# Sums of squares of x and mem taken from their columns by products with ones

## The chip, the cores and the metric

The kernel runs on one core of one Trainium2 chip. The metric is the device time of one execution in microseconds (us). Engines: PE (TensorE; PEld is its weight load), ACT (ScalarE), DVE (VectorE), POOL (GpSimd), SP (SyncE, which here only issues loads and stores).

## What is computed

One decoder layer on 256 tokens of width 1024, in float32. What matters here is its first step: x and 256 memory tokens mem are normalised by rows (RMSNorm) and projected.

```
def rmsnorm(x, g):
    y = x * rsqrt(mean(x * x, axis=-1) + EPS)
    return y * g

h = rmsnorm(x, mix_norm_g)                      # (256, 1024)
proj = h @ w_in                                 # q, k, v of two attentions, mem q, 3 branch gates
mem_n = rmsnorm(mem, mem_norm_g)                # (256, 1024)
mk, mv = split(mem_n @ w_mem_kv)
# three attentions; their outputs, times sigmoid(gates), are merged and projected
x = x + merged @ w_out
x = x + ConvFFN(rmsnorm(x, ffn_norm_g))
```

## The kernel before

Every weight is split into a rounded part (hi, by ACT) and the rest (lo, by DVE or by a DMA of POOL that adds), and so is every activation. A product of the reference is three products on PE: hi by hi, hi by lo, lo by hi. Weights come from DRAM in pieces of up to 512 KB into 6 raw slots; a raw slot is free when its lo part is made, and there are 6 slots for the hi and lo parts, free when PE has used them.

x is loaded twice: transposed (`x_cols`, tile sig, 8 blocks of 128x256), scaled by the gain and split into T_x, which PE multiplies; and by rows (tile xs, 2 blocks of 128 tokens), from which come the sums of squares and to which the layer's output is added. mem likewise: `mem_cols` gives T_mem, the rows of mem only the sums. The 1/rms of a row is applied after the projection. A row's sum of squares is made in two halves by ACT and DVE with an accumulator (tile junk), added on DVE, raised to -1/2 on POOL, and kept in tile rs. For x it is also spread along the free axis into tile R by a product of ones with a diagonal matrix (tp_R).

The program's order is written by a planner (class Order) as the kernel is built: each task is a sequence of stages on engines, with times from a cost table and priorities, and the planner writes the stage that can start first. Each engine then runs its instructions in that order, and waits where an operand is late. The order of projections is va, vd, qa, gate 0, ka, gates 1 and 2, mv, mk and so on; tiles are named after them (raw_, hi_, lo_, acc_). While PE would wait early on, the planner writes fillers (warm, products of ones with ones). The planner's cost of an fp32 product on PE is its columns times four:

```
            return n * (4 if out_parts(args) == 128 else 2) / 2400.0
```

All loads except the adding ones are issued by SP, in the order of the string LOADS at the start, and then piece by piece as slots come free (L301).

Of the kernel before, what the change touches and what calls it, by code (L numbers as in the profile page):

```python
# [11 lines left out]
F32 = mybir.dt.float32  # L12
# [3 lines left out]
AF = mybir.ActivationFunctionType  # L16
ALU = mybir.AluOpType
# [3 lines left out]
P = 128  # L21
S = 256
NT = 2
D = 1024
KT = D // P
DH = 64
# [5 lines left out]
EPS = 1e-6  # L32
# [5 lines left out]
RAW = 3  # L38
PRIO_SCALE = 11
CUTS = (0, 1, 2, 4, 8)  # L40
LOADS = "x01 g w x12 w x24 w x46 w x68 w r0 r1 c"
SUMS = (4, 130, 5)
BACK = (1.5, 2.0)
SLACK = 0.6
MEM_AT = 16.0
PRIO_SPLIT = (0, 0, 0, 12, 12, 22, 35, 40)
MAGIC = 12582912.0
TWO_PI = float(np.nextafter(np.float32(2.0 * np.pi), np.float32(0.0)))
# [185 lines left out]
def tile_layer(ctx: ExitStack, tc: tile.TileContext, io, out):  # L234
    nc = tc.nc
    od = Order(nc)
    pe, act, dve, pool = od.pe, od.act, od.dve, od.pool

    cpool = ctx.enter_context(tc.tile_pool(name="cpool", bufs=1))
# [8 lines left out]
    def bank_free(tag):  # L248

        return lambda: users[tag][-BANKS[tag]]["end"] if len(users[tag]) >= BANKS[tag] else 0.0  # L250

    def bank(tag, name):
        use = {"end": None}
        users[tag].append(use)
        shape = [P, 2, 512] if tag == "sc" else [P, 512]
        return ps.tile(shape, F32, tag=tag, name=name, bufs=BANKS[tag]), use
# [33 lines left out]
    at = {"unit": 0, "raw": 0, "dma": 0.0, "sw": 0.0, "lo": 0, "quiet": False}  # L290
# [94 lines left out]
    def urgency(part):  # L385
        def f():
            g = next((g for g in grains if (g.get("hi", {"end": None})["end"] is None if part == 0 else not g.get("taken"))), None)
            d = g["first"] - at["unit"]
            return PRIO_SPLIT[min(d, len(PRIO_SPLIT) - 1)] if d >= 0 else PRIO_SPLIT[0]
        return f  # L390
# [16 lines left out]
    xs = cpool.tile([P, NT, D], F32, tag="xs", name="xs")  # L407
# [6 lines left out]
    mhalf = cpool.tile([P, 8], F32, tag="mhalf", name="mhalf")  # L414
    ones = cpool.tile([P, P], F32, tag="ones", name="ones")
    R = cpool.tile([P, S], F32, tag="R", name="R")
    sq, rstd = {}, {}
# [5 lines left out]
    task = {}  # L423

    def done(*keys):

        return lambda: [task.get(k, {"end": None}) for k in keys]
# [11 lines left out]
    def sums(src, key, t, prio, parts):  # L439

        nm = f"{key}{t}"
        if (key, t) not in sq:
            sq[key, t] = npool.tile([P, 4], F32, tag="ssq", name="ssq_" + nm, bufs=4), []
        total, tasks = sq[key, t]
        for c0, c1, eng, after in parts:
            i = len(tasks)
            tasks.append(od.add(square_task(src, c0, c1, eng, total[:, i:i + 1], nm, after), prio))

    def rstd_task(key, t):

        total, tasks = sq[key, t]
        rs = rstd[key, t] = cpool.tile([P, 2], F32, tag=f"rs_{key}{t}", name=f"rs_{key}{t}")
        yield Stage("dve", lambda: tasks)
        dve.tensor_reduce(rs[:, 0:1], total[:, :len(tasks)], axis=AX.X, op=ALU.add)
        yield Stage("dve")
        dve.tensor_scalar(rs[:, 0:1], rs[:, 0:1], 1.0 / D, EPS, op0=ALU.mult, op1=ALU.add)
        yield Stage("pool")
        pool.tensor_tensor(rs[:, 0:1], rs[:, 0:1], mhalf[:, 0:1], op=ALU.pow)

    def head_scale_task(key, t):  # L460

        yield from rstd_task(key, t)
        rs = rstd[key, t]
        yield Stage("dve")
        dve.tensor_scalar(rs[:, 1:2], rs[:, 0:1], rs[:, 0:1], 1.0 / DH, op0=ALU.mult, op1=ALU.mult)

    def row_scale_task(key, t):

        d = npool.tile([P, P], F32, tag="diag", name=f"diag_{key}{t}")
        yield Stage("dve", done(("rs", key, t)))  # L470
        dve.tensor_scalar(d, ident, rstd[key, t][:, 0:1], None, op0=ALU.mult)
        yield Stage("pe", bank_free("tp"))
        pt, use = bank("tp", f"tp_R{key}{t}")
        pe.matmul(pt[:, :P], ones, d, start=True, stop=True)
        yield Stage("act", frees=[use])
        act.activation(R[:, t * P:(t + 1) * P], pt[:, :P], AF.Copy)
# [7 lines left out]
    def columns_of(key, gi, cols, prio, after):  # L484
        for k in range(KT):
            new = od.add(column_task(key, k, cols[:, k, :], gi, after(k)), prio + 0.01 * k)
            for t in range(NT):
                task[key, t, k] = new
# [96 lines left out]
    sig = apool.tile([P, 24, S], F32, tag="sig", name="sig")  # L585
# [284 lines left out]
    for nm, arg in ORDER:  # L870
# [15 lines left out]
        else:  # L886
            br, c = arg
# [172 lines left out]
    def mem_task():  # L1060
        yield Stage("pool", MEM_AT)
        nc.sync.dma_start(conv, io["conv"])
        cols = sig[:, KT:2 * KT, :]
        rows = sig[:, 2 * KT:3 * KT, :].rearrange("p a b -> p (a b)").rearrange("p (t n) -> p t n", t=NT)
        there = []
        for out_, in_ in [(cols[:, 0:4], io["mem_cols"][:, 0:4]), (cols[:, 4:8], io["mem_cols"][:, 4:8])] + \
                [(rows[:, t, :], io["mem"][t * P:(t + 1) * P, :]) for t in range(NT)]:
            nc.sync.dma_start(out_, in_)
            at["dma"] = max(at["dma"], od.t["pool"] + 1.15) + 1.5
            there.append(at["dma"] + 1.4)  # L1070
        columns_of("mem", 2, cols, 15, lambda k: there[k // 4])
        for t in range(NT):
            sums(rows[:, t, :], "mem", t, 16, [(0, 512, "act", there[2 + t]), (512, 1024, "act", there[2 + t])])
            task["rs", "mem", t] = od.add(head_scale_task("mem", t), 14)

    def keep_busy(start):

# [11 lines left out]
    with tc.manual_schedule():  # L1089
        nc.vector.memset(ones, 1.0)  # L1090
        nc.gpsimd.memset(mhalf, -0.5)
        warm = cpool.tile([P, 1], F32, tag="warm", name="warm")
        nc.scalar.activation(warm, mhalf[:, 0:1], AF.Square)
        xcol = sig[:, 0:KT, :]
        at["dma"] = 1.9
        there = {}
        for w in LOADS.split():
            if w == "g":
                nc.sync.dma_start(gcol, io["gcol"])
                at["dma"] += 0.06  # L1100
            elif w == "w":
                load(0.0, at["raw"] + 1)
            elif w == "c":
                nc.sync.dma_start(cst, io["cst"])
                nc.sync.dma_start(pos_i, io["pos"])
                nc.sync.dma_start(hg.rearrange("p k d -> p (k d)"), io["head_gains"].to_broadcast([P, 6 * DH]))
                at["dma"] += 1.4
            elif w[0] == "x":
                k0, k1 = int(w[1]), int(w[2])
                nc.sync.dma_start(xcol[:, k0:k1, :], io["x_cols"][:, k0:k1, :])  # L1110
                at["dma"] += 0.38 * (k1 - k0)
                for k in range(k0, k1):
                    there[k] = at["dma"] + 1.2
            else:
                t = int(w[1])
                nc.sync.dma_start(xs[:, t, :], io["x"][t * P:(t + 1) * P, :])
                at["dma"] += 1.5
                there["r", t] = at["dma"] + 1.3
        load(0.0)
        make_identity(nc, ident)  # L1120
        T["x"] = tpool.tile([P, KT, 2, S], F32R, tag="T8", name="T_x")
        T["mem"] = tpool.tile([P, KT, 2, S], F32R, tag="T8", name="T_mem")
        for k in od.t:
            od.t[k] = 3.2
        warm_up = ps.tile([P, 512], F32, tag="acc", name="warm_up", bufs=4)
        for i in range(WARM):
            nc.tensor.matmul(warm_up[:, :P], ones, ones, start=True, stop=True)
        for t in range(NT):
            r = there["r", t]
            sums(xs[:, t, :], "x", t, 9, [(0, 512, "act", r), (512, 1024, "dve", r)])  # L1130
            task["rs", "x", t] = od.add(head_scale_task("x", t), 8)
            task[f"R{t}"] = od.add(row_scale_task("x", t), 9)
        columns_of("x", 0, xcol, 2, lambda k: there[k])
        od.add(split_hi(), urgency(0))
        at["left"] = len(grains)
        od.add(split_lo("dve"), urgency(1))
        od.add(split_lo("sum"), 35)
        task["mask"] = od.add(mask_task(), 25)
        od.add(mem_task(), 15)
        task["rope"] = od.add(rope_task(), 18)  # L1140
        for b in range(3):
            task[("sig", b)] = od.add(sig_task(b), 28)
        od.add(spine(units), 50)
        for key in [("out", c, t, 512) for c in range(2) for t in range(NT)]:
            while key not in task:
                od.run(units[-1])
            od.run(task[key])
# [50 lines left out]
```

## Time and profile before

| | us |
|---|---|
| median of 3 runs (419.21 to 419.32) | 419.26 |
| profiled execution | 419.38 |
| its span, first to last instruction | 417.6 |
| PE busy | 407.9 |
| DVE busy | 302.7 |
| ACT busy | 269.1 |

The times of the rows below are of the profiled execution and count from the start of its span. A DMA share of 1 or more is read as full.

### The profile page before, as it was taken

The numbers are of one execution on the slowest core, as the hardware profiler recorded it, in microseconds if no ns is written. First come the engines' busy times: TensorE is split into PE (matmuls) and PEld (weight loads), VectorE is DVE, ScalarE is ACT, GpSimd is POOL, SyncE is SP. The second block draws the span as 40 slices with busy tenths as digits, with TensorE's granted clock in tenths as the row PEclk, the third lists the DMA queues.
The fourth block names the chain that finished last, engine by engine and source line by source line (L and its number), as shares of the span: only waits on it lengthen the run. The fifth ranks groups of instructions, "written<-read, shape, count | busy, mean of one in ns | idle before, by whom it ended". The sixth has DMA issues, their size and how long they took to land.

```text
span 417.6 us, 7771 instructions
## 1 busy us (share of the span) xinstructions
PE 407.9 (98%) x2968; PEld 384.0 (92%) x2968; DVE 302.7 (72%) x600; ACT 269.1 (64%) x448; POOL 62.3 (15%) x63
## 2 busy tenths in 40 slices
PE   8899999999999999999999989999999999999996
PEld 7799999989898999999889889999999999888996
DVE  2699986586786586367987999999998778545301
ACT  4699756768976665956577877766668776433300
POOL 0101534113424102322007200000000000000000
PEclk9999999999999999999999999999999999999999
DMA  6999986667677777577597659666799688664001
GB/s 198 383 374 278 317 249 157 181 167 180 146 200 162 201 208 197 131 228 239 140 290 177 162 131 287 188 187 201 230 257 222 230 220 239 204 197 150 0 2 50
DMA packets 97988, 83.12 MB, mean 199 GB/s; under 512 B 3104, under 2 KB 85920, under 8 KB 97952
## 3 DMA queue, kind: packets, MB, share of 16 engines
q1 hardware_dynamic: 95360, 73.86, 58.6%
q0 software_dynamic: 2592, 8.78, 11.7%
q8 instruction: 23, 0.38, 0.4%
q14 instruction: 13, 0.11, 0.1%
HBM read 72.80 MB, written 1.05 MB: 177 GB/s over the span
## 4 chain that ended last, share of the span: by engine, by line
PE 83%; DVE 8%; ACT 3%; DMA 2%; issue 2%; SPq 1%; DVEq 0%; ACTq 0%
PE acc_u L101 27%; PE acc_g L101 16%; PE acc_d L101 15%; PE acc_o L101 5%; PE acc_qd L101 2%; PE acc_kd L101 2%; DMA xs<-x 2%; PE acc_ba L101 2%; PE acc_bd L101 2%; PE sc L101 2%; PE po L101 2%; PE acc_mk L101 1%; PE acc_qm L101 1%; PE acc_bm L101 1%; PE acc_mv L101 1%
## 5 line engine op out<-in xcount | busy, mean ns | idle before, releaser
L101 PE MATMUL acc_u<-T_h,hi_up 128*128 128x256 f32 x512 | 91.4, 282 | 0.0
L101 PEld LDWEIGHTS acc_u<-T_h,hi_up 128*128 128x128 f32 x512 | 78.9, 189 | 0.0
L101 PE MATMUL acc_u<-T_h,lo_up 128*128 128x256 f32 x256 | 72.1, 282 | 0.0
L101 PE MATMUL acc_g<-T_x,hi_gate 128*128 128x256 f32 x384 | 71.8, 287 | 0.0
L101 PEld LDWEIGHTS acc_g<-T_x,hi_gate 128*128 128x128 f32 x384 | 59.6, 191 | 2.4 <-issue 2.2
L101 PE MATMUL acc_d<-hi_dn,gT 128*128 128x512 f32 (+1 forms) x220 | 57.0, 348 | 0.0
L101 PE MATMUL acc_g<-T_x,lo_gate 128*128 128x256 f32 x192 | 54.2, 282 | 0.0
L101 ACT ACTIVATE hi_up<-raw_up 128x1024 fp32r<-128x1024 f32 x44 | 46.0, 1054 | 4.3 <-DMA raw_up<-w_ffn_up 1.7
L101 PEld LDWEIGHTS acc_u<-T_h,lo_up 128*128 128x128 f32 x256 | 48.4, 189 | 0.0
L101 DVE TENSOR_TENSOR lo_up<-raw_up,hi_up 128x1024 fp32r<-128x1024 f32 x39 | 47.6, 1232 | 0.0
L101 DVE SCALAR_TENSOR_TENSOR y<-acc_u,conv,y 128x255 f32<-128x255 f32 x88 | 42.2, 481 | 7.3 <-ACT y L101 5.4
L101 PEld LDWEIGHTS acc_d<-hi_dn,gT 128*128 128x128 f32 x220 | 38.5, 189 | 5.5
L101 PE MATMUL acc_d<-lo_dn,gT 128*128 128x512 f32 (+1 forms) x110 | 38.3, 348 | 0.0
L101 DVE TENSOR_TENSOR lo_dn<-raw_dn,hi_dn 128x1024 fp32r<-128x1024 f32 x21 | 25.7, 1224 | 17.3 <-ACT hi_dn L101 17.3
L101 ACT ACTIVATE hi_dn<-raw_dn 128x1024 fp32r<-128x1024 f32 x22 | 23.3, 1057 | 22.4 <-PE acc_d L101 22.4
L101 PE MATMUL acc_u<-T_hu,hi_up 128*128 128x256 f32 x192 | 34.9, 284 | 2.6 <-DVE y L101 2.6
L101 PEld LDWEIGHTS acc_g<-T_x,lo_gate 128*128 128x128 f32 x192 | 36.7, 191 | 0.0
L101 DVE TENSOR_TENSOR lo_gate<-raw_gate,hi_gate 128x1024 fp32r<-128x1024 f32 x19 | 23.8, 1262 | 13.3 <-ACT hi_gate L101 12.8
L101 PEld LDWEIGHTS acc_u<-T_hu,hi_up 128*128 128x128 f32 x192 | 29.6, 189 | 2.9 <-ACT T_h L101 2.9
L101 ACT ACTIVATE y<-acc_u,conv 128x256 f32<-128x256 f32 x44 | 24.4, 561 | 10.9 <-PE acc_u L101 10.3
L101 ACT ACTIVATE hi_gate<-raw_gate 128x1024 fp32r<-128x1024 f32 x24 | 25.0, 1056 | 6.1 <-PE acc_qm L101 2.9
L101 PE MATMUL acc_u<-T_hu,lo_up 128*128 128x256 f32 x96 | 27.1, 282 | 0.0
(279 smaller groups left out, 850.9 us busy)
## 6 DMA issues: line engine op xcount, KB each, us to landing
raw_up<-w_ffn_up SPq DMA_DIRECT2D x44, 512.0 KB, 5.1
raw_gate<-w_in SPq DMA_DIRECT2D x24, 512.0 KB, 5.2
raw_dn<-w_ffn_down SPq DMA_DIRECT2D x22, 512.0 KB, 4.4
raw_wo<-w_out SPq DMA_DIRECT2D x8, 512.0 KB, 5.2
lo_gate<-raw_gate POOLq DMA_DIRECT2D x5, 512.0 KB, 5.1
lo_up<-raw_up POOLq DMA_DIRECT2D x5, 512.0 KB, 5.0
raw_vd<-w_in SPq DMA_DIRECT2D x4, 384.0 KB, 6.6
raw_qa<-w_in SPq DMA_DIRECT2D x4, 384.0 KB, 7.7
```

What stands on the lines that cost most here:

```text
L101: return fn(*args, **kw)
```

## The change

The sums of squares of x and of mem are made from the columns: ACT squares the 8 blocks in two passes of 128x1024 into a free part of sig; PE multiplies, for each of 2 row blocks and 8 column blocks, the squares as 128x128 weight with one column of ones (16 products, sums on PSUM, tile tp_s); DVE and POOL make the scales of both row blocks at once. The rows of mem aren't loaded any more. The rows of x are loaded when the planner's clock is at 110. The columns of x are issued on ACT's queue, ahead of its table load, the last four blocks in one load.

```diff
-LOADS = "x01 g w x12 w x24 w x46 w x68 w r0 r1 c"
+LOADS = "x01 g w x12 w x24 w x48 w w w c"
+ROWS_AT = 110.0
+SQUARES_AT = 12.5
...
+    def column_square_task(cols, out_, k0, k1, after):
+        yield Stage("act", after, SQUARES_AT)
+        act.activation(out_[:, k0:k1, :], cols[:, k0:k1, :], AF.Square)
+
+    def scales_of(key, cols, squares, prio, there):
+        tasks = [od.add(column_square_task(cols, squares, k, k + 4, there[k + 3]), prio) for k in (0, 4)]
+        new = od.add(column_scale_task(key, squares, tasks), prio)
+        for t in range(NT):
+            task["rs", key, t] = new
+
+    def column_scale_task(key, squares, tasks):
+        rs = cpool.tile([P, NT, 2], F32, tag=f"rs_{key}", name=f"rs_{key}")
+        for t in range(NT):
+            rstd[key, t] = rs[:, t, :]
+        yield Stage("pe", bank_free("tp"), lambda: tasks)
+        pt, use = bank("tp", f"tp_s{key}")
+        for t in range(NT):
+            for k in range(KT):
+                pe.matmul(pt[:, t:t + 1], squares[:, k, t * P:(t + 1) * P], ones[:, 0:1], start=k == 0, stop=k == KT - 1)
+        yield Stage("dve", frees=[use])
+        dve.tensor_scalar(rs[:, :, 0], pt[:, 0:NT], 1.0 / D, EPS, op0=ALU.mult, op1=ALU.add)
+        yield Stage("pool")
+        pool.tensor_tensor(rs[:, :, 0], rs[:, :, 0], mhalf[:, 0:NT], op=ALU.pow)
+        yield Stage("dve")
+        dve.scalar_tensor_tensor(rs[:, :, 1], rs[:, :, 0], 1.0 / DH, rs[:, :, 0], op0=ALU.mult, op1=ALU.mult)
...
-        for out_, in_ in [(cols[:, 0:4], io["mem_cols"][:, 0:4]), (cols[:, 4:8], io["mem_cols"][:, 4:8])] + \
-                [(rows[:, t, :], io["mem"][t * P:(t + 1) * P, :]) for t in range(NT)]:
-            nc.sync.dma_start(out_, in_)
+        for k in (0, 4):
+            nc.sync.dma_start(cols[:, k:k + 4], io["mem_cols"][:, k:k + 4])
...
-            sums(rows[:, t, :], "mem", t, 16, [(0, 512, "act", there[2 + t]), (512, 1024, "act", there[2 + t])])
-            task["rs", "mem", t] = od.add(head_scale_task("mem", t), 14)
+        scales_of("mem", cols, sig[:, 2 * KT:3 * KT, :], 16, there)
+
+    def rows_task():
+        yield Stage("pool", ROWS_AT)
         for t in range(NT):
+            nc.sync.dma_start(xs[:, t, :], io["x"][t * P:(t + 1) * P, :])
...
-        nc.scalar.activation(warm, mhalf[:, 0:1], AF.Square)
...
-                nc.sync.dma_start(xcol[:, k0:k1, :], io["x_cols"][:, k0:k1, :])
+                nc.scalar.dma_start(xcol[:, k0:k1, :], io["x_cols"][:, k0:k1, :])
...
+        nc.scalar.activation(warm, mhalf[:, 0:1], AF.Square)
...
-            sums(xs[:, t, :], "x", t, 9, [(0, 512, "act", r), (512, 1024, "dve", r)])
-            task["rs", "x", t] = od.add(head_scale_task("x", t), 8)
-            task[f"R{t}"] = od.add(row_scale_task("x", t), 9)
+        scales_of("x", xcol, sig[:, 2 * KT:3 * KT, :], 11, there)
+            task[f"R{t}"] = od.add(row_scale_task("x", t), 12)
+        od.add(rows_task(), 30)
```

PE at the end of va and the start of vd, before (acc_va and acc_vd are the PSUM sums of the two projections, T_x the split columns of x, warm the fillers):

```order
L101 MATMUL acc_va_162<-hi_va_0_213,T_x 128x384
L101 MATMUL tp_Rx_261<-diag_x_129,ones 128x128
L1086 MATMUL warm_16.205137333333333_279<-ones 128x128 x4
L101 MATMUL tp_Rx_284<-diag_x_132,ones 128x128
L1086 MATMUL warm_17.89915200000002_294<-ones 128x128 x6
L101 MATMUL acc_vd_301<-hi_vd_0_276,T_x 128x384
```

The same place now:

```order
L103 MATMUL tp_sx<-ones,sig 128x1 x16
L103 MATMUL acc_va_156<-hi_va_0_207,T_x 128x384
L103 MATMUL acc_va_156<-lo_va_0_208,T_x 128x384
L103 MATMUL acc_va_156<-hi_va_0_207,T_x 128x384 x2
L103 MATMUL acc_va_156<-lo_va_0_208,T_x 128x384
L103 MATMUL acc_va_156<-hi_va_0_207,T_x 128x384
L103 MATMUL acc_vd_278<-hi_vd_0_222,T_x 128x384
L103 MATMUL acc_vd_278<-lo_vd_0_223,T_x 128x384
L103 MATMUL acc_vd_278<-hi_vd_0_222,T_x 128x384 x2
L103 MATMUL acc_vd_278<-lo_vd_0_223,T_x 128x384
L103 MATMUL acc_vd_278<-hi_vd_0_222,T_x 128x384
L103 MATMUL tp_Rx_293<-diag_x_125,ones 128x128
```

The 16 products stand ahead of the last six of va, the two tp_R have moved behind the first six of vd, and the fillers between va and vd are gone.

PE in the middle of qa, now (before, the rows of acc_qa follow each other there with nothing between them):

```order
L103 MATMUL acc_qa_404<-lo_qa_0_328,T_x 128x384
L103 MATMUL acc_qa_404<-hi_qa_0_327,T_x 128x384
L103 MATMUL tp_smem<-ones,sig 128x1 x16
L103 MATMUL acc_qa_392<-hi_qa_0_339,T_x 128x384
L103 MATMUL acc_qa_392<-lo_qa_0_340,T_x 128x384
```

The sums of mem stand behind the second of four pieces of qa.

SP, its first loads, before:

```order
L1110 DMA sig<-x_cols 128x256
L1099 DMA gcol<-gcol 128x24
L301 DMA raw_va_0_95<-w_in 128x384
L1110 DMA sig<-x_cols 128x256
L301 DMA raw_va_0_98<-w_in 128x384
L1110 DMA sig<-x_cols 128x512
L301 DMA raw_va_0_101<-w_in 128x2x384
L1110 DMA sig<-x_cols 128x512
L301 DMA raw_va_0_104<-w_in 128x2x384
L1110 DMA sig<-x_cols 128x512
L301 DMA raw_va_0_107<-w_in 128x2x384
L1116 DMA xs<-x 128x1024 x2
```

SP now, from its start to the columns of mem:

```order
L1124 DMA gcol<-gcol 128x24
L303 DMA raw_va_0_94<-w_in 128x384
L303 DMA raw_va_0_97<-w_in 128x384
L303 DMA raw_va_0_100<-w_in 128x2x384
L303 DMA raw_va_0_103<-w_in 128x2x384
L303 DMA raw_va_0_105<-w_in 128x2x384
L303 DMA raw_vd_0_107<-w_in 128x2x384
...
L303 DMA raw_qa_0_234<-w_in 128x2x384
L303 DMA raw_qa_0_276<-w_in 128x2x384
L1085 DMA conv<-conv 128x176
L1089 DMA sig<-mem_cols 128x1024 x2
```

The four loads of x_cols are at the head of ACT's list instead; the columns of mem now stand behind all four pieces of qa, before they stood behind two.

## Rows read from the trace of the kernel before

**Rows 1.** The page's busy line: busy us (share of the span) xinstructions.

```profile
PE 407.9 (98%) x2968; PEld 384.0 (92%) x2968; DVE 302.7 (72%) x600; ACT 269.1 (64%) x448; POOL 62.3 (15%) x63
```

**Rows 2.** Stretches: us; busy (xinstructions) per engine; granted clock, DMA share, GB/s.

```profile
0.00:4.00 4.00, 2.94 (x14) 2.94 (x15) 0.24 (x2) 2.00 (x3) 0.74 (x7) 1.00 0.41 110
4.00:7.00 3.00, 2.69 (x12) 2.05 (x11) 1.37 (x3) 1.22 (x3) 0.00 (x0) 1.00 0.71 179
7.00:13.70 6.70, 5.62 (x31) 4.73 (x31) 4.06 (x7) 4.53 (x9) 0.00 (x0) 1.00 1.03 362
18.20:21.70 3.50, 2.79 (x24) 2.74 (x24) 1.64 (x6) 2.35 (x7) 0.55 (x1) 1.00 1.07 373
21.70:51.70 30.00, 30.00 (x189) 29.65 (x187) 29.14 (x70) 26.12 (x45) 6.30 (x6) 1.00 1.02 324
55.00:110.00 55.00, 55.00 (x431) 51.25 (x431) 38.25 (x94) 39.32 (x78) 18.20 (x14) 1.00 0.69 187
```

**Rows 3.** PE's timeline: start us, us, engine, line, operation [idle before <-releaser].

```profile
17.89 0.34 PE L101 MATMUL acc_va<-hi_va,T_x 128*128 128x384 f32 x1
...
21.73 0.42 PE L101 MATMUL acc_vd<-hi_vd,T_x 128*128 128x384 f32 x1
...
30.24 0.33 PE L101 MATMUL acc_qa<-hi_qa,T_x 128*128 128x384 f32 x1
...
52.42 0.55 PE L101 MATMUL tp_qa<-ident,t_qa 128*128 128x128 f32 x3 [0.66 <-DVE t_qa L101]
```

**Rows 4.** The timeline of PE's weight loads, merged where they follow each other.

```profile
1.05 1.78 PEld L1127 LDWEIGHTS warm_up<-ones 128*128 128x128 f32 x8 [1.05 <-DVE ones L1090]
2.72 2.25 PEld L1086 LDWEIGHTS warm_5.374288_148<-ones 128*128 128x128 f32 x10
4.95 0.28 PEld L101 LDWEIGHTS acc_va<-hi_va,T_x 128*128 128x128 f32 x1
...
20.37 1.42 PEld L1086 LDWEIGHTS rm_17.89915200000002_294<-ones 128*128 128x128 f32 x12
21.71 0.19 PEld L101 LDWEIGHTS acc_vd<-hi_vd,T_x 128*128 128x128 f32 x1
...
88.78 0.63 PEld L101 LDWEIGHTS po<-pT,v_va 128*64 128x64 f32 x8 [0.17 <-issue]
```

**Rows 5.** ACT's timeline.

```profile
0.74 1.28 ACT L1093 ACT_TABLE_LOAD   x1 [0.74 <-PEq L1190]
2.03 0.20 ACT L1093 ACTIVATE warm<-mhalf 128x1 f32<-128x1 f32 x1
4.37 0.52 ACT L101 ACTIVATE hi_va<-raw_va 128x384 fp32r<-128x384 f32 x1 [0.48 <-DMA raw_va<-w_in]
...
11.03 0.91 ACT L101 ACTIVATE T_x<-sig,gcol 128x256 fp32r<-128x256 f32 x2 [0.62 <-DMA sig<-x_cols]
12.05 0.85 ACT L101 ACTIVATE hi_va<-raw_va 128x768 fp32r<-128x768 f32 x1
...
25.75 3.31 ACT L101 ACTIVATE T_mem<-sig,gcol 128x256 fp32r<-128x256 f32 x8 [0.50 <-DMA sig<-mem_cols]
...
29.58 0.56 ACT L101 ACTIVATE v_vd<-acc_vd,rs_x 128x384 f32<-128x384 f32 x1
```

**Rows 6.** SP's last issue for va; landings of raw_va; issues of mem_cols (last: us to landing).

```profile
5.81 0.49 SPq L301 DMA_DIRECT2D raw_va<-w_in  x1
...
DMA to landing us min/median/max: 2.7/6.0/7.9
...
sig<-mem_cols SPq DMA_DIRECT2D x2, 512.0 KB, 8.2
```

**Rows 7.** The page's costliest groups: a pass of ACT over 128x1024.

```profile
L101 ACT ACTIVATE hi_gate<-raw_gate 128x1024 fp32r<-128x1024 f32 x24 | 25.0, 1056 | 6.1 <-PE acc_qm L101 2.9
```

**Rows 8.** Tile lo_vd: duration ns min/median/max, first and last start.

```profile
L101 DVE TENSOR_TENSOR lo_vd<-raw_vd,hi_vd x4: 954/958/960, 21.0 to 24.0; 128x768 fp32r<-128x768 f32 x4
```

**Rows 9.** Tile xs: its first use behind the sums.

```profile
L101 DVE TENSOR_TENSOR xs<-acc_o,xs x5: 414/692/692, 209.8 to 223.9; 128x512 f32<-128x512 f32 x3, 128x256 f32<-128x256 f32 x2
```

More of the change, by code (lines that the diff above doesn't have):

```diff
@@ L458, in rstd_task @@
         pool.tensor_tensor(rs[:, 0:1], rs[:, 0:1], mhalf[:, 0:1], op=ALU.pow)
-    def head_scale_task(key, t):
-        yield from rstd_task(key, t)
-        rs = rstd[key, t]
+    def column_square_task(cols, out_, k0, k1, after):
[19 more added lines that the diff above has]
+        pool.tensor_tensor(rs[:, :, 0], rs[:, :, 0], mhalf[:, 0:NT], op=ALU.pow)
         yield Stage("dve")
-        dve.tensor_scalar(rs[:, 1:2], rs[:, 0:1], rs[:, 0:1], 1.0 / DH, op0=ALU.mult, op1=ALU.mult)
+        dve.scalar_tensor_tensor(rs[:, :, 1], rs[:, :, 0], 1.0 / DH, rs[:, :, 0], op0=ALU.mult, op1=ALU.mult)
     def row_scale_task(key, t):
@@ L1063, in mem_task @@
         cols = sig[:, KT:2 * KT, :]
-        rows = sig[:, 2 * KT:3 * KT, :].rearrange("p a b -> p (a b)").rearrange("p (t n) -> p t n", t=NT)
         there = []
-        for out_, in_ in [(cols[:, 0:4], io["mem_cols"][:, 0:4]), (cols[:, 4:8], io["mem_cols"][:, 4:8])] + \
-                [(rows[:, t, :], io["mem"][t * P:(t + 1) * P, :]) for t in range(NT)]:
-            nc.sync.dma_start(out_, in_)
+        for k in (0, 4):
+            nc.sync.dma_start(cols[:, k:k + 4], io["mem_cols"][:, k:k + 4])
             at["dma"] = max(at["dma"], od.t["pool"] + 1.15) + 1.5
-            there.append(at["dma"] + 1.4)
-        columns_of("mem", 2, cols, 15, lambda k: there[k // 4])
+            there += [at["dma"] + 1.4] * 4
+        columns_of("mem", 2, cols, 15, lambda k: there[k])
+        scales_of("mem", cols, sig[:, 2 * KT:3 * KT, :], 16, there)
+    def rows_task():
+        yield Stage("pool", ROWS_AT)
         for t in range(NT):
-            sums(rows[:, t, :], "mem", t, 16, [(0, 512, "act", there[2 + t]), (512, 1024, "act", there[2 + t])])
-            task["rs", "mem", t] = od.add(head_scale_task("mem", t), 14)
+            nc.sync.dma_start(xs[:, t, :], io["x"][t * P:(t + 1) * P, :])
+            at["dma"] = max(at["dma"], od.t["pool"] + 1.15) + 1.5
     def keep_busy(start):
@@ L1113, in tile_layer @@
                     there[k] = at["dma"] + 1.2
[L1114 to L1118, printed above, removed]
+        nc.scalar.activation(warm, mhalf[:, 0:1], AF.Square)
         load(0.0)
@@ L1127, in tile_layer @@
             nc.tensor.matmul(warm_up[:, :P], ones, ones, start=True, stop=True)
+        columns_of("x", 0, xcol, 2, lambda k: there[k])
+        scales_of("x", xcol, sig[:, 2 * KT:3 * KT, :], 11, there)
         for t in range(NT):
-            r = there["r", t]
-            sums(xs[:, t, :], "x", t, 9, [(0, 512, "act", r), (512, 1024, "dve", r)])
-            task["rs", "x", t] = od.add(head_scale_task("x", t), 8)
-            task[f"R{t}"] = od.add(row_scale_task("x", t), 9)
-        columns_of("x", 0, xcol, 2, lambda k: there[k])
+            task[f"R{t}"] = od.add(row_scale_task("x", t), 12)
+        od.add(rows_task(), 30)
         od.add(split_hi(), urgency(0))
@@ L1172 @@
         "x": arr(x).reshape(S, D),
-        "mem": arr(mem).reshape(S, D),
         "x_cols": arr(np.asarray(x).reshape(S, KT, P).transpose(2, 1, 0)),
```

## Prediction

> **What bounds the kernel now.** I read the page's busy line first, then the stretches, then PE's timeline. PE is busy for 98% of the span, and 92% of it has a weight load running [rows 1]. The stretches show where that holds: from 21.7 to 51.7 PE is busy 30.00 of 30.00 us, and from 55 to 110 again 55.00 of 55.00 [rows 2]. So whatever PE gains or loses before 55 us arrives whole at the end; work on the other engines counts only where PE waits for it. There are two such places. In the opening, the first projection (va) ends at 18.23, and the second (vd) starts at 21.73 [rows 3]: between them PE runs fillers and two small products while the sums of squares of x go through ACT, DVE and POOL. The other is 0.66 us before tp_qa at 52.42, where DVE is late [rows 3]. The opening is short of data: the DMA engines are busy 1.03 from 7 to 13.7 and 1.07 from 18.2 to 21.7, but only 0.71 from 4 to 7 [rows 2].
>
> **Part 1: data and the start of vd.** By 13.7 the last va weights had landed (issued at 5.81, longest landing 7.9 [rows 6]). By then 0.44 + 0.54 + 2.43 = 3.40 MB had moved [rows 2]. What va needs is 1.05 MB of x columns, 1.57 MB of weights and the gains: 2.63 MB. The other 0.77 MB were rows of x and constants; the rows no longer run there, which at 362 GB/s is 2.1 us, so 11.6. The second queue can at most fill the idle DMA share from 4 to 7, 0.29 x 3 = 0.9 us: 10.7. If the queues share evenly, the 1.05 MB of x columns are in while 0.52 MB of va are not, 1.45 us earlier: 9.2 to 10.2. I take 9.2, since DMA engines that stand idle with loads waiting point to the single queue.
>
> By the Trainium skill ("DMA: Bandwidth & Descriptors", section "Issuing engines are not separate DMA queues") loads issued by several engines run on the same 16 DMA engines, and a second issuer saves only the time of issuing. By it the columns land at 10.2, not 9.2, and the sum below is 1.0 us higher. The low share from 4 to 7 [rows 2] neither shows nor excludes that.
>
> ACT now issues four loads before its table load: 4 x 0.43 (one issue on SP took 0.37 to 0.49, [rows 6]), so its first T_x starts at 0.74 + 1.7 + 1.28 + 0.2 = 3.95 [rows 5]. It costs nothing: the step behind that T_x now waits until 4.37 for weights [rows 5], and 3.95 + 0.45 + 0.52 gives the first product at 4.9, as now (4.95, [rows 4]).
>
> From 9.2 ACT has three T_x (0.45 each), a hi_va (0.85), a T_x, a hi_va, a hi_vd, and the two squares of 128x1024, which the trace lacks; nearest is a 128x1024 pass with 1.06 [rows 5, 7]. 1.35 + 0.85 + 0.45 + 1.7 + 2.1 = 6.45: squares at 15.7. PE has all of va but its last six products done at about 15.5 (lo of the last piece but one at 9.2 + 1.35 + 0.85 + 0.96 = 12.4, then 18 products of 0.177) and waits for the squares. Then the 16 products with ones. Each is fp32 with a new 128x128 weight and one column; the trace has none. An fp32 product runs as two passes, each with its own load. The six fillers at 20.37, also 128x128 fp32, have 12 loads in 1.42 us, with starts from 20.37 to 21.71 = 0.112 each [rows 4]. Not their 128 columns set that, since po's products, of 128 and 256 columns but with half the weight, come faster (below): the loads do, and one column doesn't shorten a load. So 32 x 0.112 = 3.6 us. Below: the loads of po, 64 columns wide, come every 0.63/8 = 0.079, 2.5 us. Above: loads that don't overlap at all, 0.19 each (a single load of 128x128, [rows 4]), 6.1 us. I take 3.6, the same form of load. So 15.7 + 3.6 = 19.3, six products at 8.51/48 = 0.177 [rows 3] end at 20.35, and vd starts there: 21.73 - 20.35 = 1.4 us gained. Ends: if ACT never waits for data, squares are done at 3.95 + 10.1 = 14.1 and vd starts at 18.8 (2.9 gained); with columns no sooner than 11.03, as now [rows 5], at 22.1 (0.4 lost).
>
> **Part 2: moved into vd.** The two products that spread 1/rms of x over R stood in the wait; now they stand between products of vd: 2 x 2 passes x 0.112 = 0.45 us lost.
>
> **Part 3: sums of mem.** Another 16 products in the middle of qa, where PE has no idle time: 3.6 us lost (2.5 to 6.1). They take from ACT four half-row squares and put two whole ones there, and take some eight small steps from DVE; both hide under PE. But PE now waits there for ACT. I count from X, the end of the sums of x. DVE makes the scale and one lo_vd (0.96, [rows 8]); that frees the slot of the last qa load, and the mem columns are issued by X + 3. They and that load are 1.5 MB, at 373 GB/s 4.1 us, with some 2 us until the first lands (the shortest landing is 2.7, [rows 6]): X + 9. ACT then has three T_mem (0.41), two v_vd (0.57), a T_mem and two squares [rows 5, 7]: 1.2 + 1.1 + 0.4 + 2.1, so X + 13.9. PE is there after six va, vd, the 0.45 and half of qa: 1.05 + 8.51 + 0.45 + 4.25 = X + 14.3. It fits by 0.4 us.
>
> **Part 4: the stall at tp_qa.** Those transposes now stand behind all of ka, so PE reaches them later relative to DVE, which has lost work: 0.66 us gained. Next late would be lo_ka of the last ka piece, now made by ACT and a POOL DMA; by the same count from X it has over 2 us.
>
> **Hidden.** The rows of x, 1.05 MB = 2.8 us of DMA, go out among the ba weights, past 100 us; the DMA share up to 110 is 0.69 [rows 2], and the rows are read only at 210 [rows 9]. Uncovered they would cost those 2.8 us.
>
> **Sum.** -1.4 + 0.45 + 3.6 - 0.66 = +2.0 us. The profiled execution took 419.38 (span 417.6); the median of the runs is 419.26, 0.1 lower. I forecast 421.3; all times here stand on the median. With the ends of part 1 alone it is 419.8 to 423.1.
>
> **Rivals.**
> Cheap sums: faster. If an fp32 product with one column needs only one load, or the load is halved, a set takes 1.8 us: vd starts at 18.55, and the sum is 2.0 - 2 x 1.8 = -1.6: 417.7. For it: the trace has no product of one column, and loads of 64 columns are quicker [rows 4]. Against: loads of the same shape and type hold 0.112. It decides below 2.6 us a set, where the sum is nil.
>
> Mem columns late: with the 8.2 us to landing that they take now [rows 6], they are there at X + 11.2, the squares at X + 16.1, and PE waits 1.8 us: 423.1. For it: they are issued behind more loads than now. Against: the DMA has less queued by then, since 2 MB are gone.
>
> The clock falls. The granted clock reads 1.00 (2.4 GHz) in every stretch [rows 2], though the same 128x128 loads came every 0.22 us before the first projection and every 0.112 later [rows 4], so a slow phase is not excluded. If 3.6 us of one-column products bring that phase back, for as long as the opening had it (1.05 to 4.95, [rows 4]), half of 3.9 is lost: 1.95 each time, 423.3 after one set, 425.2 after both. Against: PE's fillers and short gaps elsewhere leave the column at 1.00. The Trainium skill ("TensorE: Matmul & The Clock Gate", section "What's actually happening") says that the gate goes back to 1.2 GHz when PE was little busy, and (section "Part 4: PE-mode transpose") that a transpose doesn't count as busy in the same way; whether one-column products count, no run here shows.
>
> **Chances.** Forecast 0.5 (own range 419.8 to 422.6), cheap sums 0.2, late mem columns 0.17, clock 0.13. A change of 0.2%, 0.8 us, is about what a measurement of this kernel can tell from none. Of the forecast's 0.5 some 0.08 lie within that, of cheap sums 0.06: faster 0.15, the same 0.15, slower 0.7. Leaving a tenth out at each end gives 418.3 to 424.0.
>
> **What would show it.** Right: vd starts near 20.3, each set of 32 loads takes 3.4 to 3.8 us, tp_smem starts without a wait behind the first half of qa, ka ends some 2 us later than before, and PE has no idle time from there to 110. Wrong: a set under 2.6 us, vd before 18.8, idle time of PE before tp_smem, or a granted clock under 1.00. The forecast as a whole fails most easily on the price of one fp32 product with a single column, since it counts twice.

## The result and the profile after

The changed kernel takes 431.1 us (median of 4 runs, 427.91 to 431.39) against 419.24 before: 1.027 times as long, 95% interval 1.022 to 1.031. The forecast was 421.3, the range ended at 424.0. The profiled execution took 431.39 (span 429.6, 12.0 more than before), so it stands for the median. Medians here and below leave out two slow executions, one of the kernel before (442.38, clock 0.853) and one of e6_bcast (566.59, 0.656).

The page's busy line, as in [rows 1]: PE has 12.5 us more to do, the other engines no more than before. The loss is on PE itself.

```profile
PE 420.4 (98%) x3016; PEld 397.2 (92%) x3016; DVE 299.4 (70%) x588; ACT 269.1 (63%) x440; POOL 62.2 (14%) x61
```

Stretches, PE alone (us, busy and instructions, granted clock, DMA share, GB/s); the first three answer to [rows 2]:

```profile
4.00:7.00 3.00, 2.37 (x9) 1.00 0.96 300
21.70:51.70 30.00, 30.00 (x160) 0.80 0.75 221
55.00:110.00 55.00, 53.58 (x403) 1.00 0.74 196
...
20.00:22.00 2.00, 2.00 (x12) 0.58 0.06 12
22.00:24.00 2.00, 2.00 (x7) 0.50 0.01 3
24.00:26.00 2.00, 2.00 (x8) 0.50 0.93 272
26.00:28.00 2.00, 2.00 (x11) 0.71 0.95 280
28.00:30.00 2.00, 2.00 (x14) 1.00 0.99 317
...
40.00:42.00 2.00, 2.00 (x15) 0.70 0.68 193
42.00:44.00 2.00, 2.00 (x8) 0.50 0.73 210
44.00:46.00 2.00, 2.00 (x7) 0.50 0.53 153
46.00:48.00 2.00, 2.00 (x9) 0.59 0.88 254
```

From 21.7 to 51.7 PE is as busy as before, 30 of 30 us, yet with 160 instructions in place of 189. The last column but two says why: the clock falls twice to 0.50 (1.2 GHz of 2.4), from about 20 to 28 and from about 40 to 48. The missing clock adds up to 2 x (0.42 + 0.50 + 0.50 + 0.29) = 3.42 us of PE's time the first time, 2 x (0.30 + 0.50 + 0.50 + 0.41) = 3.42 the second. A busy column alone hides this.

PE's timeline (start, us), the rows that answer to [rows 3], and the two sets:

```profile
5.90 0.69 PE L103 MATMUL acc_va<-hi_va,T_x 128*128 128x384 f32 x1 [0.63 <-ACT hi_va L103]
...
6.98 0.84 PE L103 MATMUL acc_va<-hi_va,T_x 128*128 128x384 f32 x2
...
10.37 1.50 PE L1112 MATMUL warm_8.807152_177<-ones 128*128 128x128 f32 x12
...
12.23 0.51 PE L103 MATMUL acc_va<-hi_va,T_x 128*128 128x384 f32 x2
...
17.55 4.28 PE L103 MATMUL tp_sx<-ones,sig 128*128 128x1 f32 x32
21.69 0.67 PE L103 MATMUL acc_va<-hi_va,T_x 128*128 128x384 f32 x1
...
23.76 0.52 PE L103 MATMUL acc_vd<-hi_vd,T_x 128*128 128x384 f32 x1
...
34.13 0.34 PE L103 MATMUL acc_qa<-hi_qa,T_x 128*128 128x384 f32 x1
...
63.83 0.55 PE L103 MATMUL tp_qa<-ident,t_qa 128*128 128x128 f32 x3 [1.42 <-DVE t_qa L103]
```

Each fall begins inside a set of one-column products (17.55 to 21.8) and outlasts it: the products of va at 21.69 take 0.67 where [rows 3] have 0.34.

The opening was slow as well: up to about 10 us two products of va take 0.84 us, later 0.51, and this the clock column (1.00 from 4 to 7) does not show. It cost nothing: in e2_one_block, below, such a pair takes 0.51 from 6.45 on, and PE reaches the first set at 17.47, here at 17.55.

PE's weight loads, as in [rows 4]:

```profile
17.38 4.37 PEld L103 LDWEIGHTS tp_sx<-ones,sig 128*128 128x128 f32 x32
25.36 1.08 PEld L103 LDWEIGHTS tp_Rx<-diag_x,ones 128*128 128x128 f32 x4
38.12 4.61 PEld L103 LDWEIGHTS tp_smem<-ones,sig 128*128 128x128 f32 x32
```

ACT's timeline, as in [rows 5], and raw_va's landings, as in [rows 6]:

```profile
5.33 0.52 ACT L103 ACTIVATE hi_va<-raw_va 128x384 fp32r<-128x384 f32 x1 [0.81 <-DMA raw_va<-w_in]
...
7.65 0.53 ACT L103 ACTIVATE hi_va<-raw_va 128x384 fp32r<-128x384 f32 x1 [1.40 <-DMA raw_va<-w_in]
...
10.06 0.84 ACT L103 ACTIVATE hi_va<-raw_va 128x768 fp32r<-128x768 f32 x1 [1.09 <-DMA raw_va<-w_in]
10.81 1.29 ACT L103 ACTIVATE T_x<-sig,gcol 128x256 fp32r<-128x256 f32 x3
...
14.61 1.99 ACT L103 ACTIVATE sig<-sig 128x1024 f32<-128x1024 f32 x2
...
35.20 2.00 ACT L103 ACTIVATE sig<-sig 128x1024 f32<-128x1024 f32 x2
```
```profile
DMA to landing us min/median/max: 4.1/7.2/7.9
```

ACT waits three times for va's weights (0.81, 1.40, 1.09) and not for the columns. The squares of mem end at 37.2, before tp_smem: PE does not wait there.

Laid end to end, by the starts of the projections, the profiled executions differ so: va and vd, up to the start of qa, 34.13 - 30.24 = +3.9, of which 3.4 is clock; qa 15.1 against 8.3 = +6.8, of which 3.4 is clock and the rest the set; the wait at tp_qa +0.8. That is 11.4 at the first product of mv; another 0.6 comes piecemeal up to the end.

### The profile page after: what moved, and what is told of

The parts are those of the page before. It is cut to its first block, busy times and chain, and to the rows that moved or that the text cites. A ratio compares the mean times of both kernels' runs of the same rounds, so it can differ in the third digit from the quotient of the medians.

```text
span 429.6 us, 7845 instructions
## 1 busy us (share of the span) xinstructions
PE 420.4 (98%) x3016; PEld 397.2 (92%) x3016; DVE 299.4 (70%) x588; ACT 269.1 (63%) x440; POOL 62.2 (14%) x61
## 4 chain that ended last, share of the span: by engine, by line
PE 93%; DVE 2%; ACT 2%; DMA 1%; issue 0%; SPq 0%; ACTq 0%
PE acc_u L103 26%; PE acc_g L103 16%; PE acc_d L103 14%; PE acc_o L103 5%; PE acc_va L103 3%; PE acc_qa L103 2%; PE acc_vd L103 2%; PE acc_bd L103 2%; PE acc_ba L103 2%; PE acc_qd L103 2%; PE acc_kd L103 2%; PE sc L103 2%; PE po L103 2%; PE acc_qm L103 1%; PE acc_mk L103 1%; PE acc_bm L103 1%
```

## The experiments

The kernel before took 419.0 to 419.3 in each series. Where a mean clock is given, 1 less the clock, times the span, is at most the PE time lost to it: 0.984 in the changed kernel is 6.9 us, 0.992 (its run of 427.91) 3.4. It counts falls in the opening and behind PE's last product too, which cost nothing. Only one run of each kernel is profiled; where the clock fell in the others is inferred.

**1. As many products, 128 columns each (e1_wide).**

```diff
-    pe.matmul(pt[:, t:t + 1], squares[:, k, t * P:(t + 1) * P], ones[:, 0:1], ...)
+    nc.tensor.matmul(pt[:, t * P:(t + 1) * P], squares[:, k, t * P:(t + 1) * P], ones, ...)
-    dve.tensor_scalar(rs[:, :, 0], pt[:, 0:NT], 1.0 / D, EPS, ...)
+    dve.tensor_scalar(rs[:, :, 0], pt[:, 0:NT * P:P], 1.0 / D, EPS, ...)
```

> The changed kernel with 128 columns of ones in each of the 32 products of the sums instead of one (column 0 is read); same order, same 64 passes, same weight loads. Theory A (the clock falls because the one-column products leave PE all but idle, and the products behind them then run at half the clock for 6.84 us each time): granted clock 1.00 throughout, a set still 3.4 to 3.8 us, and 2 x 3.4 us less: 424.3 us, or 423.5 if the longer wait of DVE before tp_qa goes too. Theory B (the 64 passes and their waits cost the time, the clock reading is a by-product): a set as long as in the changed kernel, 4.1 to 4.4 us or longer, 431 us.

425.27 us, ratio 1.015 (1.013 to 1.017): 5.8 us less than the change, with the same 64 weight loads and 128 times the columns. Its timeline at the sets and at tp_qa, and stretches in the opening and behind the sets:

```profile
17.54 3.73 PE L482 MATMUL tp_sx<-ones,sig 128*128 128x128 f32 x32
...
35.41 3.73 PE L482 MATMUL tp_smem<-ones,sig 128*128 128x128 f32 x32
...
57.77 0.55 PE L103 MATMUL tp_qa<-ident,t_qa 128*128 128x128 f32 x3 [1.43 <-DVE t_qa L103]
```
```profile
5.00:10.00 5.00, 3.60 (x12) 0.75 1.01 374
...
20.00:22.00 2.00, 2.00 (x18) 1.00 0.00 1
...
40.00:42.00 2.00, 2.00 (x14) 1.00 0.94 266
```

The clock stays at 1.00 behind both sets; its fall in the opening costs nothing, since PE is at the first set at 17.54, as in the change. So the falls come with the single column, not with the loads, whose number is the same, and both together are worth some 6 us. The wait at tp_qa is unchanged, 1.43.

**2. An eighth of the products (e2_one_block).**

```diff
-            for k in range(KT):
-                pe.matmul(..., start=k == 0, stop=k == KT - 1)
+            for k in range(1):
+                pe.matmul(..., start=k == 0, stop=True)
```

> The changed kernel with only the first of 8 blocks of columns in each sum: 2 products a set instead of 16 (the sums leave out 7 of 8 blocks; times of everything else stand). Takes the sets away and with them the low activity. Theory A and B agree on the sets: 431.1 - 2 x 3.0 (passes left out at full clock) - 6.8 (falls) = 418.3, clock 1.00. What it tells apart is the rest of the change: if loads on two queues and no rows bring vd forward, as the prediction had it, vd starts at 18.0 or sooner and the time is 416.5 or less; if the va weights are no sooner than before, va still ends near 18.5, vd starts at 18.9, and the time is 417.5 to 418.5.

418.96 us, ratio 0.9993 (0.998 to 1.000). A set takes 0.50 us. Its timeline at tp_qa:

```profile
51.38 0.55 PE L103 MATMUL tp_qa<-ident,t_qa 128*128 128x128 f32 x3 [1.43 <-DVE t_qa L103]
```

With the sets almost gone the change is worth nothing. vd starts at 18.98, 2.7 us sooner than before; 0.45 goes to tp_R, 0.5 to the second set, 0.77 to the longer wait at tp_qa, which leaves 1.04 at tp_qa (51.38 against 52.42), 0.6 at PE's last product and 0.2 in the span.

**3. Squares added up first, two products a set (e3_presum).** DVE adds the 8 blocks of x, POOL those of mem.

```diff
+        if key == "x":
+            dve.tensor_reduce(total, squares.rearrange("p k s -> p s k"), axis=AX.X, op=ALU.add)
...
+        else:                                       # n = 4, 2, 1
+            pool.tensor_tensor(squares[:, 0:n, :], squares[:, 0:n, :], squares[:, n:2 * n, :], op=ALU.add)
```

> The changed kernel with the squares of the 8 blocks added first (x by one reduction on DVE, mem by three additions on POOL), then 2 products of one column a set; complete computation. If the number of products on PE is what matters (both theories), it comes out like the kernel with one block, within 0.7 us: 417.5 to 418.5, clock 1.00. If the reduction on DVE (2048 elements, some 2.2 us) delays the split of vd, vd has a wait of PE of 1 to 2 us and the time is 419 to 420.

426.23 us, ratio 1.017 (1.014 to 1.019): a miss. The additions took time of engines that others wait for. PE's longest wait, and the stretches around it:

```profile
53.84 0.44 PE L104 MATMUL acc_ka<-lo_ka,T_x 128*128 128x384 f32 x1 [4.02 <-DMA lo_ka<-raw_ka]
```
```profile
50.00:55.00 5.00, 1.14 (x5) 0.99 0.55 122
55.00:60.00 5.00, 2.73 (x10) 0.50 1.03 288
```

The trace gives this chain, untested: while POOL adds (32.06 to 37.73) DVE's steps stretch (one took 2.43 us, the same step 0.21 at 40.53); ACT then waits 4.01 us for a gate's weights and makes its part of lo_ka at 46.77; POOL waits for that and issues the adding DMA at 47.92, in e2 at 41.86. PE waits 4.0 us for it, and the clock is at 0.50 in the stretch after. So a fall can follow idle time of PE as well.

**4. The same eighth, x columns on SP's queue again (e4_one_block_sp).**

```diff
-LOADS = "x01 g w x12 w x24 w x48 w w w c"
+LOADS = "x01 g w x12 w x24 w x46 w x68 w w c"
...
-                nc.scalar.dma_start(xcol[:, k0:k1, :], ...)
+                nc.sync.dma_start(xcol[:, k0:k1, :], ...)
```

> As the kernel with one block, but the columns of x are issued by SP between the va weights, as before the change, and the table load of ACT stands first again (rows of x and mem still not loaded early; sums leave out 7 of 8 blocks). Theory C (columns of x on a second queue take DMA time from the first va weights): the second and third va weights land 0.5 to 1 us sooner, va ends at 17 to 17.7, and it is 0.5 to 1.2 us faster than the kernel with one block: 416.5 to 417.5. Rival (the second queue brings data sooner, as the prediction had it): 0.5 to 1 us slower than the kernel with one block.

420.04 us, ratio 1.002 (1.001 to 1.003). ACT's table load stands first again as well. The first product is at 5.09 (5.58 in e2) and vd starts at 18.14 in place of 18.98; 0.37 of this are four filler passes that e2 has in va and this order has not, the rest va's weights, which the columns on ACT's queue do hold up. But PE then waits 2.54 us at tp_qa, with the clock at a mean of 0.68 from 50 to 55, and the end is no sooner: the four runs at a mean clock of 0.999 or more took 418.8 to 419.4, the six below it 420.0 to 421.0.

**5 and 6. One set wide, one of single columns (e5_x_wide, e9_mem_wide).**

```diff
+    n = P if key == "x" else 1                      # e9_mem_wide: "mem"
+    nc.tensor.matmul(pt[:, t * P:t * P + n], squares[:, k, t * P:(t + 1) * P], ones[:, 0:n], ...)
```

> The changed kernel with 128 columns of ones in the products on x and one column, as in the change, in those on mem. From the kernel with 128 columns in both (425.27 us, clock 1.00 behind both sets) and the changed kernel (431.1, two stretches of 6.84 us at 0.50). Theory A, each set of one-column products brings one fall of the clock, and each fall costs half of 6.84 = 3.4 us of PE's time: a set of one column is 0.3 us shorter at full clock (3.45 against 3.73), so 425.3 - 0.3 + 3.4 = 428.4, with 1.00 behind tp_sx and one stretch at 0.50 behind tp_smem. Theory B, the first fall is what matters and brings the second (by the later start of all that follows): no fall, 425.0. Theory C, the fall in the middle of qa is the dear one and the first is hidden by the wait for x's scale: 431.

> The counterpart of e5_x_wide: one column of ones in the products on x, as in the change, and 128 in those on mem. Theory A, the set on x brings a fall of the clock by itself, as it did in the changed kernel: the kernel with 128 columns in both took 425.3, a set of one column is 0.3 us shorter, a fall costs 3.4: 428.4, with a stretch at 0.50 behind tp_sx alone. Theory B, a fall comes only where both sets are of one column: 425.0 in most runs, as with e5_x_wide (425.1, one run of four at 428.9).

| | set of one column | mean clock of each run | us of each run |
|---|---|---|---|
| e5_x_wide | mem | 0.999, 0.999, 0.999, 0.988 | 425.07, 425.14, 424.73, 428.91 |
| e9_mem_wide | x | 0.992, 0.991, 0.999, 0.995 | 427.74, 427.15, 425.20, 426.44 |

The profiled run of each, behind its set of single columns, e5_x_wide first:

```profile
40.00:42.00 2.00, 2.00 (x13) 1.00 0.99 278
```
```profile
20.00:22.00 2.00, 2.00 (x10) 0.50 0.00 0
22.00:24.00 2.00, 2.00 (x8) 0.50 0.25 25
24.00:26.00 2.00, 2.00 (x10) 0.50 0.98 321
26.00:28.00 2.00, 2.00 (x12) 0.81 0.93 278
```

Neither theory holds as put. One set can bring a fall by itself (e9's profiled run), so two aren't needed; but a set doesn't bring it in every run (e5's profiled run has none). Read by mean clock and time, there was none in three of four runs of e5 and in one of four of e9. Runs without one take 424.7 to 425.2 (with both sets wide 425.1 to 425.3, and one of 426.64 at 0.996); those with one 426.4 to 428.9. What decides it the runs don't show.

**7 and 8. Ones as the weight, 256 columns of squares (e6_bcast), and its transposes later (e7_bcast_late).** The squares are rounded to fp32r in a tile of their own; every partition gets all 256 sums, and DVE takes its own with the identity.

```diff
+        for k in range(KT):
+            pe.matmul(pt[:, 0:S], ones_r, squares[k // 4][:, k % 4, :], start=k == 0, stop=k == KT - 1)
+        for t in range(NT):
+            dve.scalar_tensor_tensor(junk, pt[:, t * P:(t + 1) * P], 1.0 / D, ident, op0=ALU.mult, op1=ALU.mult, accum_out=rs[:, t, 0:1])
```

> The changed kernel with the sums turned round: ones (128x128, fp32r) are the weight and eight blocks of 256 squares (fp32r) stream past them, one pass each, the sums then taken from the diagonal by two DVE operations of 128x128 with the identity. Eight products at 0.12 us (the price of the 256-column fp32r products of the gates) make 0.96 us a set in place of 3.45 and more. Theory A (length of the sets and clock are the whole loss): the kernel with an eighth of the products took 418.96 with 0.50 us a set, so 418.96 + 2 x 0.46 = 419.9, and up to 0.7 more if DVE's two longer steps delay vd; clock 1.00 throughout. Theory B, 256 columns cost twice as much with a new weight each time (0.24): 421.8. Theory C, something else in the new order costs time (the eighth of the products hid it): over 422.

419.33 us, ratio 1.001 (1.000 to 1.002). The sets in its timeline:

```profile
17.48 1.11 PE L103 MATMUL tp_sx<-squares,ones_r 128*128 128x256 f32 x8
...
31.42 1.30 PE L103 MATMUL tp_smem<-squares,ones_r 128*128 128x256 f32 x8
```

They take 1.11 and 1.30 where e1's take 3.73 each: 5.05 us less on PE, and 5.2 less in the profiled executions (420.08 against 425.32; 5.9 by the medians). The price of the sets arrives whole. PE doesn't wait at tp_qa here, but 1.57 us at a gate product (39.76) for a low part that POOL's DMA adds.

```diff
+    r += LATE if e == "pe" and task["gen"].__name__ == "post_task" else 0.0      # LATE = 2.0
```

> The kernel of e6_bcast, with the transposes behind q and k planned 2 us later, so that those of qa stand behind all of ka and eight gate products rather than six ka products before its end. Theory A, the lead won in the opening is lost at tp_qa (1.43 us idle there in the kernel with an eighth of the products), and PE has other work to put there: e6_bcast less 1.0 to 1.4, so about 418.6. Theory B, DVE itself is behind, and the wait comes back at the next thing that DVE makes (the low parts of the gate weights or tp_ka): the same as e6_bcast within 0.3.

428.76 us, 9 slower than e6_bcast, at a clock of 0.988 to 1.000.

**9. The same later transposes in the kernel before (e8_before_late).**

> The kernel before with the same later transposes and nothing else. Theory A: its 0.66 us at tp_qa are gone, 419.05 - 0.66 = 418.4. Theory B: the wait comes back elsewhere, 419.0 to 419.2.

427.39 us, ratio 1.019 (1.018 to 1.021). Three stretches:

```profile
50.00:55.00 5.00, 5.00 (x38) 1.00 0.80 184
105.00:115.00 10.00, 8.57 (x50) 1.00 0.22 69
180.00:200.00 20.00, 17.07 (x135) 1.00 0.72 184
```

The wait at tp_qa is gone (50 to 55 is full; 4.34 busy before), and more than it comes back in the attention steps, where the kernel before had no idle time (10.00 of 10 us busy from 105 to 115, 20.00 of 20 from 180 to 200). The later transposes also changed which low parts the planner gives to POOL. In the trace PE waits there for ACT (pT, three waits, 2.9 us) and DVE (oT, 1.5), for no low part; but what made these late I did not separate.

**10. e6_bcast with the x columns on SP (e10_bcast_sp)**, the diff of experiment 4.

> The kernel of e6_bcast (419.5) with the x columns issued by SP between the weights, as in the kernel before. Theory A, ACT's queue costs the first va weights 0.9 us, and DVE has the room: 418.6. Theory B, vd starts sooner but the lead is lost again at tp_qa, where DVE bounds (2.54 us of idle PE there in e4_one_block_sp): 419.3 to 420.0.

419.07 us, ratio 1.000 (0.999 to 1.001), with 1.48 us of idle PE at tp_qa.

**11. The part on mem alone, in the kernel before (e11_mem_only).**

```diff
-        rows = sig[:, 2 * KT:3 * KT, :] ...         # the rows of mem, their loads and their sums
+        scales_of("mem", cols, sig[:, 2 * KT:3 * KT, :], 16, there)
```

> The kernel before with one part of the change alone: the sums of mem by 16 one-column products, its rows not loaded; x stays as before. From the prediction's part 3, with the set's own duration at full clock (3.45): 419.0 + 3.45 = 422.5, or 421.8 if those 3.45 us also take PE to tp_qa later and so swallow the 0.66 us of waiting there. Theory A, the clock falls behind it in every run: 425.2 to 425.9. Theory B, the set alone leaves the clock at 1.00, as on mem in e5_x_wide: 421.8 to 422.5 in most runs.

426.17 us, ratio 1.016 (1.014 to 1.018), clock 0.991 to 0.994 in all four runs. The profiled run behind the set (36.0 to 39.5):

```profile
38.00:40.00 2.00, 2.00 (x17) 0.84 0.72 193
40.00:42.00 2.00, 2.00 (x8) 0.50 0.47 131
42.00:44.00 2.00, 2.00 (x13) 0.80 0.89 256
```

Laid end to end as above: vd starts 0.53 us sooner (21.20), qa takes 13.47 against 8.32, which is 5.15 more and of it 2 x (0.16 + 0.50 + 0.20) = 1.72 clock, and the wait at tp_qa is 0.75 longer (1.41): +5.4 there, +5.5 in the span (423.1). The other runs took up to 1.0 us more at a lower mean clock. Part 3 of the change makes more than half of the loss by itself.

**12. e10_bcast_sp with qa's transposes alone behind ka (e12_bcast_sp_late).**

```diff
-            yield Stage("pe", bank_free("tp"))
+            yield Stage("pe", bank_free("tp"), od.t["dve"] + (LATE if nm == "qa" else 0.0))      # LATE = 0.4
...
-                return g if SUMS[0] <= g["id"] < SUMS[1] and ...
+                return g if g["piece"]["key"][0] != "mk" and SUMS[0] <= g["id"] < SUMS[1] and ...
```

> The kernel of e10_bcast_sp with the transposes of qa alone planned 0.4 us later, which puts the first of them behind all of ka; and the low parts of the mk weights are kept off POOL's queue (the later order put them there, as in e8_before_late, 427.4). Theory A, the idle time at tp_qa goes and nothing else does: 1.4 to 2.5 us under e10_bcast_sp, about 417.8. Theory B, the wait only moves, to the gate products or to the attention steps at 95 to 200 us, as in e8_before_late: the same as e10_bcast_sp or up to 8 us slower.

418.75 us, ratio 0.9989 (0.998 to 1.000): 0.43 us idle at tp_qa, but 0.95 now at tp_ka (70.34). The wait mostly moved, in the profiled run at least, which is the slowest of the ten (419.99). It is the lowest median, and at the edge of what can be told from no change.

## Why the prediction was wrong

The direction held, the size did not: +2.0 was forecast, +12.0 measured in the profiled execution. By the prediction's own terms:

| term | forecast | measured | how |
|---|---|---|---|
| clock | 0 | +6.84 | two falls of 3.42 |
| parts 1 and 2, clock taken out | -0.95 | +0.47 | 34.13 - 30.24 - 3.42 |
| part 3 | +3.6 | +3.3 | qa 15.08 - 8.32 - 3.42 |
| part 4 | -0.66 | +0.76 | 1.42 - 0.66 |
| after the first product of mv | 0 | +0.6 | 12.0 - 11.4 |

**The clock** is the step that failed, with 6.84 of the 10.0 us missed. It stood as a rival at 0.13 and 1.95 us a fall. Both numbers came from reading the wrong rows. "PE's fillers and short gaps elsewhere leave the column at 1.00" was taken as evidence for the sets, but the fillers stream 128 columns, and in e1 the same sets with 128 columns left the clock at 1.00. The price came from the spacing of loads in the opening, where the granted clock reads 1.00, and which in the changed kernel lasts to about 10 us and not 4.95; a fall measured here is 6.84 us at half clock, 3.4 lost. By the Trainium skill ("TensorE: Matmul & The Clock Gate", section "What's actually happening") the gate follows how busy PE was of late, and its monitor runs free of the kernel's start. Here PE's busy column is full as the clock falls (2.00 of 2.00 us from 20 to 22), so that column alone gives no warning; that the same set brings a fall in one run and none in another (e5, e9) agrees with a monitor that runs free, though no run shows that this is why.

**Part 1.** vd starts at 23.76, and at 22.16 where the clock holds (e1), not at 20.35. The columns came early enough: the last load of them landed at about 9.8 (issued at 2.1, 7.7 us), between the prediction's 9.2 and 10.2, ACT makes three T_x at 10.81 without a wait, and the squares are done at 16.6 (15.7 forecast). But PE was not at the set by 15.5: it got there at 17.55. I had va bounded by the columns, [rows 5] showing ACT waiting for one; with them early, va waits for its weights. Though issued sooner they take longer to land (median 7.2 us, 6.0 before), and the first three pieces reach ACT later (hi_va at 5.33, 7.65 and 10.06; before 4.37, 6.70 and 9.57). The first product comes at 5.90 and not 4.9, and in e2, where PE is at full pace, its last wait in va is for the third piece's low part, until 11.87 (11.46 before). Fillers stand at 10.37 and 13.97. The DMA share from 4 to 7 rose to 0.96, but the first weights were no sooner for it. What was next late behind the stall I removed was the thing to ask; e4 prices the second queue, with the fillers that came with it, at 0.84 us of vd's start.

**Part 2** costs about what was forecast (the four loads of tp_R took 1.08, but at half clock).

**Part 3** was right in its own term: at full clock a set takes 3.63 us (tp_smem in e5_x_wide) against 3.6, with the slow stretch 4.28 (tp_sx) and 4.52 (tp_smem); e11 shows the part alone.

**Part 4** rested on a misreading: six products of ka still stand behind tp_qa, so nothing covers it. The wait is 1.41 to 1.43 in the changed kernel, e1, e2, e5, e9 and e11, whether PE gets there at 51 or at 64. It hangs on PE's own gate 0, behind which ka follows. DVE in the changed kernel, before the first transposes of qa, and then the same steps before:

```profile
56.73 1.48 DVE L103 TENSOR_TENSOR lo_gate<-raw_gate,hi_gate 128x1024 fp32r<-128x1024 f32 x1 [1.24 <-ACT hi_gate L103]
...
60.44 1.22 DVE L103 TENSOR_TENSOR lo_gate<-raw_gate,hi_gate 128x1024 fp32r<-128x1024 f32 x1
...
63.16 0.61 DVE L103 SCALAR_TENSOR_TENSOR t_qa<-t_qa,rs_x,hs_qa 128x384 f32<-128x384 f32 x1
```
```profile
51.75 0.61 DVE L101 SCALAR_TENSOR_TENSOR t_qa<-t_qa,rs_x,hs_qa 128x384 f32<-128x384 f32 x1
52.28 1.22 DVE L101 TENSOR_TENSOR lo_gate<-raw_gate,hi_gate 128x1024 fp32r<-128x1024 f32 x1
```

The low part at 60.44 (1.13 us to the next step) now stands ahead of the last t_qa; before it stood behind it, at 52.28. And DVE waits at 56.73 for a hi_gate that ACT makes only after its pass over gate 0, so the chain starts with PE's own work there. From the first product of ka to tp_qa it is 8.88 us now (54.95 to 63.83), 8.88 in e2, 8.11 before. That is the low part's 1.13 less 0.36 that DVE is ahead at the first t_qa (58.13 - 54.95 against 47.85 - 44.31). A lead won in the opening passes this place less 0.77. The reason is read from the traces and not tested: e12 moves the transposes (0.43 us of wait left there), not DVE's steps.

**The rivals.** Cheap sums fell (3.63 us a set at full clock). Late mem columns fell: tp_smem starts without a wait. The clock was the right mechanism at half its price; had it been sized at 3.4 a fall, that rival would have read 428.1 with both falls, and 431.0 with parts 1, 2 and 4 as measured. The range failed with it: it ended at 424.0, below the clock's own 425.2.

## What to carry to other kernels

Price a new matmul twice: by its weight loads, and by what it does to the clock. Products of one column, back to back for 3.6 us, could take PE to half clock here, and the bill is paid by the dense work behind them; evidence that the clock holds should come from products of the same shape. If the sum runs along the partitions, make ones the weight and let the data stream (1.1 to 1.3 us here in place of 3.6 to 4.5, and no fall behind the sets in the profiled runs of e6 and e10). Behind every stall that a change removes, ask which operand is late next.

## What the runs showed of the hardware

- A set of 32 fp32 passes with one column took 3.63 us at full clock (e5_x_wide), with 128 columns 3.73: 0.11 to 0.12 a pass either way.
- Behind one-column sets the profiled runs show the granted clock at 0.50 for 6.84 us (the change, twice, and e9) or 3.4 us (e11), and once not at all (e5); behind the same sets with 128 columns it read 1.00 each time (e1, e5, e9). By mean clock and time, how often it fell varied between places (one of four runs to four of four).
- After 4.0 us of waiting, with PE busy 1.14 of 5 us, the clock fell to 0.50 (e3), and after 2.54 us to a mean of 0.68 (e4); after 1.43 it stayed at 1.00 (e2), though in e1's opening it fell behind a wait of 1.50.
- A DVE step of 128x128 took 2.43 us while POOL added 128x1024 blocks, and 0.21 later (e3).
